# Moving sixteen accumulating transfers of a weight sum from the attention stage into the recurrence stage of a hybrid block

## Chip, cores and metric

The kernel runs on one core of one Trainium2 chip. The metric is the time of one execution on the device in microseconds (us), taken as the median of several runs. All other times are from one profiled execution.

## What is computed

One layer on 1024 tokens of width 1024: a stick-breaking attention (8 heads of 64) and a gated linear recurrence, HGRN2 (4 heads of 128), run on the same normalised input, are merged by two sigmoid gates, and are followed by an MLP and a norm.

```python
xn = rmsnorm(x, norm1_g[layer])
u = xn @ w_in[layer].astype(f32)
q_sb, k_sb, v_sb, f_raw, i_hg, q_hg, g_hg, gate_sb, gate_hg = jnp.split(u, list(c), axis=-1)
o_sb = stick_breaking_attention(...)
o_hg = hgrn2_chunkwise(...)          # state: S_t = diag(f_t) S_{t-1} + k_t v_t^T
o_hg = merge_heads(rmsnorm(o_hg, ...)) * jax.nn.silu(g_hg)
g_a = jax.nn.sigmoid(gate_sb + bg[:D_MODEL])
g_b = jax.nn.sigmoid(gate_hg + bg[D_MODEL:])
merged = g_a * (o_sb @ w_o_sb) + g_b * (o_hg @ w_o_hg)
h = x + merged @ w_out
h = h + jnp.square(jax.nn.relu(rmsnorm(h, norm2_g) @ w_ff1)) @ w_ff2
return rmsnorm(h, final_g)
```

## The kernel before

Products are made in two-way split form: an operand is cast to a high part (`hi_copy`, ScalarE, L157) and the rest is subtracted into a low part (`lo_sub`, VectorE, L162); `three` issues three matmuls of 128 x 512 for one product (L129). The large products use schemes that need sums of blocks of weights. Such a sum is made in DRAM: a transfer that GpSimd issues writes a first block, and later transfers with `accum_op=add` add others to it. There are three generators of such transfers, each yielding after one issue:

- `out_weight_sums`: 32 transfers of 256 KB into `tw`, for the product with w_out (L1365).
- `sb_weight_sums`: 8 transfers of 512 KB into `tv`, for the attention's output product (L1629). Some read what an earlier one wrote.
- `gate_weight_sums`: 16 transfers of 512 KB into `tg4` (called tg in the profile, L1377). For each of four row blocks there is one plain write and then three additions, in four rounds over the four blocks. Eight raw units (`RawUnit`, wga0 to wga7) read tg4 later through SP's queue.

The stages run in this order. The attention loops over 64 `items` (8 heads of 8 query blocks, in the order 7, 0, 6, 1, 5, 2, 4, 3). For an item it issues the scans of the next (`weights`), the scores of the one after that (`scores`, z, with the sigmoid on ScalarE), some steps of the projections, the transposes (`turn`, pw, cast to wTh and wTl) and the products with the values (`values`, po). `turn` also clears a block of wTh and wTl by two GpSimd memsets when the query block is even (L892). At the end of a head GpSimd adds up the two halves of its output (osb, L941). In each item but every sixteenth one transfer of the chained generators `wsums` is issued.

The recurrence follows: for each of 4 heads `hg_levels` is a generator with eight steps, the last seven for the levels 1, 2, 4 ... 64, and `hg_tail` of the head before runs in turns with it. On a level VectorE multiplies keys (k), queries (q) and decays (pp), ScalarE copies the next keys (ksl), and TensorE makes the scores (sl). `hg_level[0]` is the product of the decays on the latest level (`mul(right, right, left)`). Between the steps the stream `st` issues steps of projections: with head 0 it is the product for i (pji, weights wir, wih, wil), whose third and fourth weight parts are split inside level 1, and the weights of f and q of head 3 (wf3, wq3) are loaded and split ahead of their use. The raw buffers of such weights are two in number, so that a load goes out once the part two before it has been split.

All loads from `load` go through SP's queue in a fixed order. `after(a, b)` adds a dependency of issue order only (`NOSYNC`). The program is put in order by a planner, which gives each engine one queue that it works off in order; on one engine nothing overtakes. GpSimd (POOL) has its transfers, memsets and the small norms of `hg_tail` (`inv_rms`, L266) in one queue.

Of the kernel before, what the change touches and what calls it, by code (L numbers as in the profile page):

```python
# [40 lines left out]
def kernel(  # L41
# [19 lines left out]
    nc = tc.nc  # L61
# [32 lines left out]
    def dram(name, shape):  # L94
        return scratch.tile(shape, F32, tag=name, name=name)
# [10 lines left out]
    def after(ins, earlier):  # L106
        if earlier is not None and earlier.ins is not ins.ins:
            tc.add_manual_dep(ins.ins, earlier.ins.name, NOSYNC, reason="issue order")
        return ins
# [710 lines left out]
    turn_lo, scored = [None], [None]  # L820

    def scores(h, qb):
        open_block("main")
        nk = (qb + 1) * P
        QH, QL, KS = qk[h]
        rm = zs[h, qb] = slot_n(f"rm{h}_{qb}", nk)
        step = 320 if nk == 640 else 512
        for s0 in range(0, nk, step):
            m = min(nk - s0, step)
            n = max(m, 256)  # L830
            z = bank(f"z{h}_{qb}_{s0}")
            for i, Q in enumerate((QH, QL)):
                matmul(
                    z[:, :n],
                    Q[:, qb * P : (qb + 1) * P],
                    KS[:, s0 : s0 + n],
                    start=i == 0,
                    stop=i == 1,
                )
            scored[0] = nc.scalar.activation(  # L840
                rm[:, s0 : s0 + m], z[:, :m], AF.Sigmoid, scale=-0.125
            )
# [7 lines left out]
    def weights(h, qb):  # L850

        nk = (qb + 1) * P
        rm = zs[h, qb]
        parts = ((512, nk), (0, 512)) if qb == NT - 1 else ((0, nk),)
        for i, (a, b) in enumerate(parts):
            rr = rm[:, a:b][:, ::-1]
            sc = nc.vector.tensor_tensor_scan(  # L859
                out=rr,  # L860
                data0=rr,
                data1=bits[:, 1024 - nk + a : 1024 - nk + b][:, ::-1],
                initial=rm[:, b : b + 1] if i else 0.0,
                op0=ALU.mult,
                op1=ALU.max,
            )
            if (h, qb) == items[0]:
                after(sc, masked[0])
            if i == 1 or (qb == 5 and h in (2,)):
                after(sc, turn_lo[0])  # L870
# [85 lines left out]
    hg_sum, hg_level = [None], [None]  # L956
# [397 lines left out]
    def out_block(i, j):  # L1354
        return W_OUT[i * 512 : (i + 1) * 512, j * 512 : (j + 1) * 512]

    def out_weight_sums():
        b11, b12, b21, b22 = (out_block(i, j) for i in range(2) for j in range(2))
        plain = ((1, b11), (3, b12), (2, b22), (4, b21))
        summed = ((1, b12), (3, b22), (2, tw[1]), (4, tw[2]))  # L1360
        for op, ways in ((ALU.bypass, plain), (ALU.add, summed)):
            for i, src in ways:
                for r in range(4):
                    rs = slice(r * P, (r + 1) * P)
                    after(nc.gpsimd.dma_start(tw[i][rs], src[rs], accum_op=op), scored[0])  # L1365
                    yield

    tg4 = dram("tg4", [512, D])

    def gate_weight_sums():  # L1370
        for op, i, c0 in (
            (ALU.bypass, 0, C_GA), (ALU.add, 0, C_GB), (ALU.add, 1, C_GA), (ALU.add, 1, C_GB),
        ):
            for r in range(4):
                rs = slice(r * P, (r + 1) * P)
                src = W_IN[i * 512 + r * P : i * 512 + (r + 1) * P, c0 : c0 + D]
                after(nc.gpsimd.dma_start(tg4[rs], src, accum_op=op), scored[0])  # L1377
                yield

    def gate_bias(which, cb):  # L1380
# [150 lines left out]
    def input_sums():  # L1531


        def step(out, a, b, op):
            after(nc.vector.tensor_tensor(out=out, in0=a, in1=b, op=op), turn_lo[0])

        def stored(m, kp, t):
            nc.gpsimd.dma_start(sx[m][kp], t)

        for kp in range(2):  # L1540
            (h00, l00), (h01, l01), (h10, l10), (h11, l11) = (
                [t.bitcast(F32) for t in xn.t[i, 2 * j + kp]] for i in range(2) for j in range(2)
            )
            s = slot(f"xs{kp}")
            step(s, h00, h10, ALU.subtract)
            yield
            step(s, s, l00, ALU.add)
            yield
            step(s, s, l10, ALU.subtract)
            stored(7, kp, s)  # L1550
            yield
            yield
            step(s, s, h11, ALU.add)
            yield
            after(
                nc.vector.scalar_tensor_tensor(
                    out=s, in0=s, scalar=-1.0, in1=l11, op0=ALU.mult, op1=ALU.subtract
                ),
                turn_lo[0],
            )  # L1560
            stored(6, kp, s)
            s4 = slot(f"xs4{kp}")
            yield
            step(s4, s, h01, ALU.add)
            yield
            step(s4, s4, l01, ALU.add)
            stored(3, kp, s4)
            yield
            step(s, s, h00, ALU.add)
            yield  # L1570
            step(s, s, l00, ALU.add)
            stored(5, kp, s)
            yield
# [41 lines left out]
    def sb_block(i, j):  # L1615
        return W_OSB[i * 256 : (i + 1) * 256, j * 512 : (j + 1) * 512]

    def sb_weight_sums():
        for t, op, src in (
            (1, ALU.bypass, sb_block(0, 0)),  # L1620
            (3, ALU.bypass, sb_block(0, 1)),
            (1, ALU.add, sb_block(0, 1)),
            (3, ALU.add, sb_block(1, 1)),
            (2, ALU.bypass, tv[1]),
            (2, ALU.add, sb_block(1, 1)),
            (4, ALU.bypass, tv[2]),
            (4, ALU.add, sb_block(1, 0)),
        ):
            after(nc.gpsimd.dma_start(tv[t], src, accum_op=op), scored[0])  # L1629
            yield  # L1630
# [1005 lines left out]
    n_first = 4  # L2636
    n_fill = n_first + 14 * NHS
    ready = deque()
    wsums = chain(out_weight_sums(), sb_weight_sums(), gate_weight_sums())
    insums = input_sums()  # L2640
    done = 0
    for i, it in enumerate(items):
        if i + 1 < len(items):
            weights(*items[i + 1])
        if i + 2 < len(items):
            st.finish(j_qk[items[min(i + 4, len(items) - 1)][0]])
            scores(*items[i + 2])
        if i < 2:
            v_moves()
        if i % 16 != 0:  # L2650
            next(wsums, None)
        if i > 2 and i % 5 > 1:
            next(insums, None)
        want = n_first + (i + 1) * (n_fill - n_first) // len(items)
        st.advance(want - done, j_q[2])
        done = want
        before = ready.popleft() if ready else None

        def between():
            if before:  # L2660
                values(*before)

        r = turn(*it, between)
        if i == len(items) - 2:
            attended[0] = turn_lo[0]
        if it[1] != NT - 1:
            between()
        if r:
            ready.append(r)
# [9 lines left out]
    for h in range(NHG + 1):  # L2679
        lev = hg_levels(h) if h < NHG else iter(())  # L2680
        tail = hg_tail(h - 1) if h > 0 else iter(())
        upto = (j_i, j_sb[0], j_raw[1], j_raw[6], j_held)[h]
        going, turned = True, False
        while going:
            going = False
            for g in (lev, tail):
                if g is tail and h == 1 and turned and going and st.pos < j_i:
                    continue
                turned = turned or g is tail
                if next(g, StopIteration) is not StopIteration:  # L2690
                    going = True
                    owed += FILL[h]
                    for step in range(int(owed)):
                        st.advance(1, upto)
                        while soon:
                            soon.pop(0)()
                    owed -= int(owed)
        if h + 1 < NHG:
            st.finish(max(j_f[h + 1], j_q[h + 1]))
# [102 lines left out]
```

## Time and profile before

| what | before |
|---|---|
| median of 3 runs | 1420.58 us (1420.08 to 1421.21) |
| profiled execution | 1421.75 us, span 1420.0 us |
| TensorE (PE) | 1406.0 us busy, 99% |
| VectorE (DVE) | 1066.9 us, 75% |
| ScalarE (ACT) | 667.8 us, 47% |
| GpSimd (POOL) | 164.4 us, 12% |
| DMA queue q1 (SP) | 196.15 MB, 40.9% of 16 engines |
| DMA queue q0 (GpSimd's) | 50.34 MB, 13.8% of 16 engines |

The span is that of the program's instructions; the execution has 1.75 us around it. Busy time of PE counts matmuls that run one into the next, so that idle time of PE is true waiting. In a row of instructions the first number is the start, the second the duration (for several, the stretch they cover), and the bracket tells how long the engine was idle before it and what ended that. In the profile tg is written from 252.1 us (first issue) to 302.0 us (last issue), and its first reader is issued at 465.4 us. The attention lasts from about 84 to 330 us.

### The profile page before, as it was taken

The page shows a single profiled execution, that of the slowest core. Times are in us where ns is not written, and L with a number is a line of the kernel's source. Part 1 is how long each engine was busy: PE and PEld are TensorE (multiplying, and loading weights), DVE is VectorE, ACT ScalarE, POOL GpSimd, SP SyncE. Part 2 cuts the span into 40 slices and gives each one's busy share as a digit, 9 for nine tenths or more (in the row PEclk, how much of TensorE's full clock was granted, in tenths as well). Part 3 has the DMA queues.
Part 4 walks back from the last instruction along what each step waited for, and adds up shares of the span by engine and source line. Part 5 has one row for each costly group of instructions (what it writes and reads, how often), then busy time and mean ns, then how long its engine had stood idle before and what let it go on. Part 6 is the DMA issues. An engine that isn't in the chain of part 4 may idle for free.

```text
span 1420.0 us, 18679 instructions
## 1 busy us (share of the span) xinstructions
PE 1406.0 (99%) x6824; PEld 1181.1 (83%) x6824; DVE 1066.9 (75%) x1463; ACT 667.8 (47%) x1147; POOL 164.4 (12%) x318
## 2 busy tenths in 40 slices
PE   9999999999999999999999999999999999999997
PEld 8888788888888888888888888888888888888886
DVE  6678887668578968987788897676666657768765
ACT  6455455554244555433334754445444443433343
POOL 3023343310001111000000300000000000000041
PEclk9999999999999999999999999999999999999999
DMA  7357778864213668364585514444346964776824
GB/s 252 83 141 201 150 142 195 211 149 134 86 56 105 215 222 264 129 215 156 165 294 194 185 59 164 163 163 149 137 143 244 355 255 160 270 278 241 282 91 176
DMA packets 169556, 258.18 MB, mean 182 GB/s; under 512 B 31404, under 2 KB 92376, under 8 KB 169432
## 3 DMA queue, kind: packets, MB, share of 16 engines
q1 hardware_dynamic: 148280, 196.15, 40.9%
q0 software_dynamic: 16320, 50.34, 13.8%
q10 hardware_dynamic: 4864, 10.49, 2.1%
q8 instruction: 54, 0.88, 0.3%
q14 instruction: 38, 0.31, 0.1%
HBM read 186.69 MB, written 84.94 MB: 191 GB/s over the span
## 4 chain that ended last, share of the span: by engine, by line
PE 95%; DVE 1%; ACT 1%; DMA 1%; issue 1%; SPq 0%; POOL 0%; POOLq 0%; DVEq 0%
PE pm L129 21%; PE pX L129 9%; PE pW L129 6%; PE pY L129 6%; PE pjqk L129 5%; PE gY L129 4%; PE gX L129 4%; PE pga L129 4%; PE pjf L129 3%; PE pji L129 3%; PE pyh L129 3%; PE pjq L129 3%; PE pys L129 3%; PE po L129 3%; PE pwX L129 2%; PE z L129 2%
## 5 line engine op out<-in xcount | busy, mean ns | idle before, releaser
L859 DVE TENSOR_TENSOR_SCAN rm<-rm,bits 128x512 f32<-128x512 f32 (+6 forms) x72 | 87.4, 1221 | 29.7 <-ACT rm L840 28.8
L157 ACT CAST whid<-w 128x1024 fp32r<-128x1024 f32 x30 | 31.6, 1054 | 154.1 <-PE pm L129 83.2
L129 PE MATMUL pm<-whid,sh 128*128 128x512 f32 x240 | 93.4, 389 | 0.0
L129 PE MATMUL pm<-wlod,sh 128*128 128x512 f32 x240 | 93.4, 389 | 0.0
L129 PE MATMUL pm<-whid,sl 128*128 128x512 f32 x240 | 93.4, 389 | 0.0
L129 PE MATMUL pm<-tl,sh 128*128 128x512 f32 (+1 forms) x210 | 81.3, 387 | 0.0
L129 PE MATMUL pm<-th,sl 128*128 128x512 f32 (+1 forms) x210 | 81.3, 387 | 0.0
L129 PE MATMUL pm<-th,sh 128*128 128x512 f32 (+1 forms) x210 | 81.3, 387 | 0.0
L162 DVE TENSOR_TENSOR wlod<-w,whid 128x1024 fp32r<-128x1024 f32 x30 | 36.7, 1223 | 53.6 <-ACT whid L157 53.6
L157 ACT CAST wTh<-pw 128x512 fp32r<-128x512 f32 (+2 forms) x96 | 43.8, 483 | 57.9 <-PE pw L132 54.2
L2413 POOL TENSOR_SCALAR fss<-fss 128x1 f32<-128x1 f32 x8 | 4.4, 552 | 562.0 <-ACT fsc L2408 561.5
L162 DVE TENSOR_TENSOR sl<-sa,sh 128x1024 fp32r<-128x1024 f32 x56 | 68.3, 1219 | 0.4 <-ACT sh L157 0.3
L162 DVE TENSOR_TENSOR wTl<-pw,wTh 128x512 fp32r<-128x512 f32 (+2 forms) x96 | 50.4, 546 | 21.8 <-ACT wTh L157 20.7
L157 ACT CAST sh<-sa 128x1024 fp32r<-128x1024 f32 x56 | 57.2, 1046 | 9.0 <-DMA sa<-ad 9.0
L129 PEld LDWEIGHTS pm<-wlod,sh 128*128 128x128 f32 x240 | 45.1, 188 | 9.5
L129 PEld LDWEIGHTS pm<-whid,sl 128*128 128x128 f32 x240 | 45.1, 188 | 9.3
L129 PEld LDWEIGHTS pm<-whid,sh 128*128 128x128 f32 x240 | 45.0, 187 | 9.4
L129 PE MATMUL pX<-sqh,t1l 128*128 128x512 f32 x128 | 49.9, 390 | 0.0
L129 PE MATMUL pX<-sql,t1h 128*128 128x512 f32 x128 | 49.9, 390 | 0.0
L129 PE MATMUL pX<-sqh,t1h 128*128 128x512 f32 x128 | 49.8, 389 | 0.0
L840 ACT ACTIVATE rm<-z 128x512 f32<-128x512 f32 (+3 forms) x96 | 44.5, 501 | 8.4 <-DMA sx<-xs 5.7
L129 PEld LDWEIGHTS pm<-th,sh 128*128 128x128 f32 x210 | 39.5, 188 | 8.1
(985 smaller groups left out, 4415.2 us busy)
## 6 DMA issues: line engine op xcount, KB each, us to landing
w<-in_w_ff_dram SPq DMA_DIRECT2D x72, 512.0 KB, 5.1
sa<-ad SPq DMA_DIRECT2D x52, 512.0 KB, 6.7
tg<-in_w_in_dram POOLq DMA_DIRECT2D x16, 512.0 KB, 9.1
ad<-a SPq DMA_DIRECT2D x32, 256.0 KB, 4.3
ad<-s SPq DMA_DIRECT2D x16, 512.0 KB, 2.8
tw<-in_w_out_dram POOLq DMA_DIRECT2D x24, 256.0 KB, 5.6
pr<-pd SPq DMA_DIRECT2D x10, 512.0 KB
x<-in_x_dram SPq DMA_DIRECT2D x8, 512.0 KB, 11.3
```

The lines of the kernel that those rows point to most:

```text
L129: return pe(nc.tensor.matmul(*a, **k))
L157: hi_last[0] = after(in_turn("act", nc.scalar.copy(dst, src)), hi_behind[0])
L162: nc.vector.tensor_tensor(out=dst, in0=src, in1=hi.bitcast(F32), op=ALU.subtract),
L840: scored[0] = nc.scalar.activation(rm[:, s0 : s0 + m], z[:, :m], AF.Sigmoid, scale=-0.125)
L859: sc = nc.vector.tensor_tensor_scan(out=rr, data0=rr, data1=bits[:, 1024 - nk + a : 1024 - nk + b][:, ::-1], initial=rm[:, b : b + 1] if i ...
L2413: nc.gpsimd.tensor_scalar(out=ssq, in0=ssq, scalar1=1.0 / D, scalar2=EPS, op0=ALU.mult, op1=ALU.add)
```

## The change

`gate_weight_sums` is taken out of the chain that the attention steps through. In the attention, the 40 transfers left are issued in 5 of 8 items and not in 15 of 16. In the recurrence, once a level has made its product of decays, one transfer of tg4 is issued after each step of `hg_levels` (for head 1 after each step of `hg_tail` too), ahead of the projection steps of that turn; its dependency of issue order is on `hg_level[0]` where it was on the latest scores. With eight steps of a head, seven transfers come with head 0 and nine with head 1. The transfers themselves are the same.

```diff
@@ gate_weight_sums
-                after(nc.gpsimd.dma_start(tg4[rs], src, accum_op=op), scored[0])
+                after(nc.gpsimd.dma_start(tg4[rs], src, accum_op=op), hg_level[0])
                 yield
@@ attention
-    wsums = chain(out_weight_sums(), sb_weight_sums(), gate_weight_sums())
+    wsums = chain(out_weight_sums(), sb_weight_sums())
+    gsums = gate_weight_sums()
...
-        if i % 16 != 0:
+        if i % 8 not in (0, 3, 6):
             next(wsums, None)
@@ recurrence
                 if next(g, StopIteration) is not StopIteration:
                     going = True
+                    if hg_level[0] and (g is lev or h == 1):
+                        next(gsums, None)
                     owed += FILL[h]
                     for step in range(int(owed)):
                         st.advance(1, upto)
```

## The prediction

> **What bounds the kernel now.** I read the page first (busy shares and the chain that ended last), then the waits of PE, then busy time by stage, then single stretches of the timeline.
>
> ```profile
> PE 1406.0 (99%) x6824; PEld 1181.1 (83%) x6824; DVE 1066.9 (75%) x1463; ACT 667.8 (47%) x1147; POOL 164.4 (12%) x318
> ...
> q0 software_dynamic: 16320, 50.34, 13.8%
> ...
> PE 95%; DVE 1%; ACT 1%; DMA 1%; issue 1%; SPq 0%; POOL 0%; POOLq 0%; DVEq 0%
> ```
> PE is busy 1406.0 of 1420.0 us and makes 95% of the chain. Only a moment in which PE stands still, or runs at a lower clock, changes the time. The stages (attention 84 to 330, first half of the recurrence 330 to 420) and the waits of PE:
>
> ```profile
> 84.00:330.00 246.00, 243.01 (x1387) 210.00 (x1386) 195.41 (x250) 137.29 (x315) 76.68 (x163) 0.99 0.73 167
> 330.00:420.00 90.00, 90.00 (x475) 76.88 (x474) 64.28 (x115) 34.08 (x73) 2.78 (x4) 1.00 0.27 88
> ...
> PE po L129 <- DVE wTl L162: 2.3, 2, 2.2
> ```
> The columns are the stretch and its length, then busy time (and count) of PE, PEld, DVE, ACT and POOL, then clock, DMA share, GB/s. The attention loses 3.0 us of PE, 2.3 of it to two waits for DVE; the recurrence loses none. The one long wait is this:
>
> ```profile
> 169.32 1.21 DVE L162 TENSOR_TENSOR wqk5l<-wqk5r,wqk5h 128x1024 fp32r<-128x1024 f32 x1
> 170.46 0.87 DVE L162 TENSOR_TENSOR wTl<-pw,wTh 128x512 fp32r<-128x512 f32 x2
> ...
> 171.18 0.39 PE L129 MATMUL po<-wTl,V 128*128 128x256 f32 x1 [2.17 <-DVE wTl L162]
> ...
> 171.00:176.00 5.00, 4.82 (x20) 4.39 (x21) 4.16 (x7) 1.72 (x4) 1.49 (x2) 0.66 0.82 213
> ```
> PE stood for 2.17 us, and in the 5 us behind it the granted clock averaged 0.66, which is 5 x 0.34 = 1.7 us more. So a stall of about 2 us costs about 3.9 in all here. No wait of PE names POOL or a DMA in the attention: the transfers that leave it were hidden there.
>
> **Removed from the attention.** Sixteen issues on POOL and 16 x 512 KB of traffic:
>
> ```profile
> L1377 POOL DMA_DIRECT2D tg<-in_w_in_dram x16: 814/1016/2087, 252.1 to 302.0; - x16
> ...
> DMA to landing us min/median/max: 6.9/9.1/12.8
> ...
> L137 SPq DMA_DIRECT2D wga0r<-tg x1: 448/448/448, 465.4 to 465.4; - x1
> ```
> 16 x 1.0 us leave POOL, which is busy 77 of 246 us there and waited for by nobody on the path: gain 0. If that cover were not there it would show as a wait of PE for POOL, and the list has none in the attention. The first reader of the sums issues at 465.4, on SP's queue; nothing below puts the last sum past 380, so that read and the loads queued behind it on SP lose nothing.
>
> **Moved within the attention.** The 32 issues for tw and 8 for tv now take 40 of the 64 items (5 in 8) where 15 in 16 took the first 42. tw ends near item 50 (only the W_OUT product behind the gates reads it: nothing). tv begins at item 52 and ends at item 63, so its chain of dependent transfers moves from 216-251 to the last head:
>
> ```profile
> 231.36 0.52 POOL L1629 DMA_DIRECT2D tv<-tv  x1 [1.03 <-DMA tv<-in_w_o_sb_dram]
> 239.47 0.91 POOL L1629 DMA_DIRECT2D tv<-in_w_o_sb_dram  x1 [7.58 <-DMA tv<-tv]
> 246.81 0.52 POOL L1629 DMA_DIRECT2D tv<-tv  x1 [4.47 <-DMA tv<-in_w_o_sb_dram]
> 251.02 0.90 POOL L1629 DMA_DIRECT2D tv<-in_w_o_sb_dram  x1 [3.04 <-DMA tv<-tv]
> ...
> 299.77 0.83 POOL L941 DMA_DIRECT2D osb<-osb  x1 [14.73 <-ACT osb L934]
> 300.31 1.15 POOL L1377 DMA_DIRECT2D tg<-in_w_in_dram  x1
> 301.14 1.46 POOL L1377 DMA_DIRECT2D tg<-in_w_in_dram  x1
> 301.98 1.75 POOL L1377 DMA_DIRECT2D tg<-in_w_in_dram  x1
> 326.97 0.82 POOL L941 DMA_DIRECT2D osb<-osb  x1 [16.38 <-ACT osb L934]
> ...
> 322.24 1.44 PE po L129 x12
> ```
> POOL waits in these. Item 58, now the tg at 301.14, becomes the first tv<-tv; with the old spacing (8.1, 7.3, 4.2 us) the second tv<-tv issues at 316.5 and the last add at 320.8. Queued behind the former on POOL are the clears of the last two attention tiles (L892); PE needs them at 322.24, so 5.7 us remain: cost 0, rival 3 if the chain is longer. The osb sum at 326.97 comes after the last add.
>
> **Added to the recurrence: the step that decides.** Each transfer is to come "behind a level's product". That dependency is of issue order. The three rows at 300.31 to 301.98 belong to items 57, 58 and 59, which are 246/64 = 3.8 us apart in PE's work, and POOL took them 0.8 us apart as soon as osb (299.77) had gone: none waited for its own activation. POOL has nothing between osb at 326.97 and the norms of the first head's tail, after 400 us, so the first four transfers go out at about 327.8 to 330, before the first level's product (332.67), and the twelve sums follow as fast as their row's last landing lets them. By bytes, 16 x 0.524 = 8.4 of q0's 50.34 MB, at 13.8% of 1420 us, is 32.7 us of all 16 DMA engines. What those engines do there already:
>
> ```profile
> 326.00:334.00 8.00, 8.00 (x37) 6.61 (x36) 7.96 (x13) 4.83 (x8) 0.82 (x1) 1.00 0.57 135
> 334.00:342.00 8.00, 8.00 (x44) 6.88 (x44) 6.76 (x10) 3.81 (x5) 0.00 (x0) 1.00 0.64 194
> 342.00:350.00 8.00, 8.00 (x41) 6.74 (x40) 7.83 (x15) 2.29 (x4) 0.00 (x0) 1.00 0.33 98
> 350.00:366.00 16.00, 16.00 (x84) 13.67 (x83) 12.01 (x23) 7.36 (x16) 0.00 (x0) 1.00 0.40 149
> ```
> That is 4.6 + 5.1 + 2.6 + 6.4 = 18.7 us of work; with 32.7 more the engines are full from 328 to about 379. Three weight loads fall into it, and they come just in time:
>
> ```profile
> 332.78 0.37 SPq L137 DMA_DIRECT2D wir<-in_w_in_dram  x1
> 334.52 0.37 SPq L137 DMA_DIRECT2D wf3r<-in_w_in_dram  x1
> 338.79 0.37 SPq L137 DMA_DIRECT2D wq3r<-in_w_in_dram  x1
> ...
> 336.26 1.06 ACT L157 CAST wih<-wir 128x1024 fp32r<-128x1024 f32 x1
> 339.21 1.05 ACT L157 CAST wf3h<-wf3r 128x1024 fp32r<-128x1024 f32 x1 [1.90 <-DMA wf3r<-in_w_in_dram]
> ...
> 332.67 0.69 DVE L170 TENSOR_TENSOR pp<-pp 128x512 f32<-128x512 f32 x1
> 337.54 1.22 DVE L162 TENSOR_TENSOR wil<-wir,wih 128x1024 fp32r<-128x1024 f32 x1
> 344.37 0.72 DVE L170 TENSOR_TENSOR q<-q,pp 128x512 f32<-128x512 f32 x1
> ...
> 345.42 1.05 PE L129 MATMUL sl<-q,ksl 128*128 128x128 f32 x8
> ```
> The last wir load lands within 336.26 - 332.78 = 3.5 us. Its cast (ACT) and its wil (DVE) stand in the queues ahead of the level's products; DVE works without a gap from 337.54 to q (ends 345.1), and PE takes that q at 345.42. The slack is 0.2 us before wil and 0.3 before PE, plus whatever the load landed before its cast, for which I choose 0.7 (the row shows no wait of ACT for it): 1.2 in all. What a load loses beside POOL's traffic:
>
> ```profile
> L137 SPq DMA_DIRECT2D wqk4r<-in_w_in_dram x2: 368/476/583, 108.9 to 109.3; - x2
> ...
> DMA to landing us min/median/max: 4.3/4.3/4.3
> ...
> L137 SPq DMA_DIRECT2D wqk6r<-in_w_in_dram x2: 368/610/852, 149.1 to 149.5; - x2
> ...
> DMA to landing us min/median/max: 8.2/8.2/8.2
> ```
> The second pair went out just behind three tw transfers (145.0 to 149.0) and took 3.9 us longer. I take 3.9: it is the same kind of load beside the same kind of traffic. Stall: 3.9 - 1.2 = 2.7 us of PE at the third level, and 1.7 for the clock as at 171: 4.4 us. The ends: nothing (the load gets through first), or 9.1 (a median tg) - 3.5 - 1.2 = 4.4 and 1.7, that is 6.1, and some 2 more if wq3r (issued at 338.79, once wir's buffer is free) adds a stall at the next level. wf3r is late by as much, but what stands behind its cast in ACT's queue (the next level's keys) waits for DVE's k, which is late already: 0. No gain can come from this step, since PE has no idle time there to win.
>
> The Trainium skill, "DMA: Bandwidth & Descriptors", section "Queues, rings and completion order", says that a DMA engine takes turns between its queues, one packet at a time; it speaks against this change. By it, as an estimate, each of wir's 16 packets per engine waits for one of q0's (0.138 x 1420 x 16 / 16320 = 0.19 us): 3.1 us later instead of 3.9, and a sum of 3.6. No view shows single packets; the 8.2 us of wqk6r are of that size. The skill's "TensorE: Matmul & The Clock Gate", "HAM oscillation", puts the gap that lowers the clock at more than about 3.4 us; here 2.17 us was followed by it, so the row is used. By the page the sum would be 2.7, inside the measurement's bound.
>
> **Sum.** The profiled execution: 1420.0 us span, 1421.75 with what lies around it, 1.17 above the median of 1420.58. Span 1420.0 + 0 (attention) + 4.4 = 1424.4; the median becomes 1425.0.
>
> **Rivals.** The least change that a measurement of this kernel can tell is taken as 0.2%, 2.8 us.
> 1. The transfers stay hidden: the loads get through, or stalls stay under 2.8 us, or each transfer really waits for its level, which spreads sixteen over 332 to 394, about 4 us apart, beside DMA shares of 0.33 to 0.64. Then 1420.6. For it: PE had no DMA wait while the same traffic ran in the attention. Against it: there wir was loaded long before its cast, here it is not. 0.37.
> 2. Faster: with sixteen entries fewer, the order in which the queues are planned in the attention comes out differently, and wqk5l no longer stands before wTl at 169.3. It decides if wTl goes first, at once after its cast: 2.2 + 1.7 = 3.9 us, 1416.7, if the recurrence adds nothing. For it: an accident of order is easily undone. Against it: neither instruction has to do with POOL. 0.17.
> 3. The tv chain holds the clears past 322.24: from a chain of over 21 us on. Four us longer than reckoned past that point, and the clock, is 5.7: 1426.3. 0.04.
> My forecast, the late load, has 0.42: between 1423.4 and 1428.6, 1425.0 the middle.
>
> Slower by over 0.2%: 0.42 + 0.04 = 0.46; within: 0.37; faster: 0.17. The range reaches from inside the faster case, 1417.2 (about 0.1 below), to 1428.6, the 8.1 us of the upper ends (0.1 above).
>
> **What would show it.** tg issues from about 328 and not at the levels' times; DMA share over 0.8 from 328 to 370; ACT idle before wih, wf3h or wq3h on a DMA for 3 us and more; PE waiting at an sl or pji matmul near 345 and a clock under 1 behind it. Wrong if PE stays at 90.0 of 90 in the recurrence, or if the time moves at 169 or in another place of the attention, where I hold the order to be as before.

## The result and the profile after

The changed kernel takes 1444.97 us (1444.71 to 1446.28, 5 runs) against 1420.08 us (1419.62 to 1421.21, 5 runs) measured beside it: ratio 1.0176, 95% interval 1.0161 to 1.0191, 24.9 us slower. The direction was the predicted one, and late weight loads are behind it as forecast; the size was 4.4 us in the forecast. The spans, 1442.8 and 1420.0 us, differ by 22.8.

The changed kernel's page, its stages, and PE's waits:

```profile
PE 1408.5 (98%) x6824; PEld 1182.2 (82%) x6824; DVE 1066.4 (74%) x1463; ACT 667.2 (46%) x1147; POOL 166.1 (12%) x318
...
q0 software_dynamic: 16320, 50.34, 13.7%
...
PE 92%; DMA 3%; DVE 2%; ACT 1%; issue 1%; POOL 0%; SPq 0%; POOLq 0%; DVEq 0%; ACTq 0%
```
```profile
84.00:330.00 246.00, 245.46 (x1406) 212.42 (x1405) 199.75 (x255) 139.67 (x317) 66.69 (x150) 1.00 0.61 137
330.00:420.00 90.00, 67.10 (x331) 56.17 (x330) 42.25 (x81) 19.46 (x36) 8.97 (x12) 0.87 0.63 160
```
```profile
PE sl L129 <- DVE q L170: 17.4, 2, 16.4
PE pji L129 <- ACT wih L157: 5.0, 1, 5.0
...
PE po L129 <- DVE wTl L162: 0.5, 2, 0.3
PE pji L129 <- DVE wil L162: 0.5, 1, 0.5
```
DMA has 3% of the chain, where it had 1%. In the recurrence PE is busy 67.1 of 90 us, where it was 90.0 of 90, with the clock at 0.87. Three stalls hold it: 5.0 us for the cast of wir (and 0.5 for wil behind it), 16.4 us for a product q, and 1.0 for the next (17.4 less 16.4). In the attention the 2.2 us at 169 are gone (0.3 is left) and the clock is 1.00. So two things moved, against each other. The osb sum that ends the attention and the first norm of the tail bound the stage:

```profile
321.86 0.82 POOL L941 DMA_DIRECT2D osb<-osb  x1 [3.47 <-ACT osb L934]
322.40 2.41 POOL L1377 DMA_DIRECT2D tg<-in_w_in_dram  x4
329.16 0.84 POOL L1377 DMA_DIRECT2D tg<-in_w_in_dram  x1 [4.35 <-DMA tg<-in_w_in_dram]
...
358.13 0.81 POOL L1377 DMA_DIRECT2D tg<-in_w_in_dram  x1 [1.98 <-DMA tg<-in_w_in_dram]
425.23 0.19 POOL L266 TENSOR_SCALAR hss<-hss 128x4 f32<-128x4 f32 x1 [66.29 <-ACT hon L1288]
```
The same norm before:

```profile
402.66 0.19 POOL L266 TENSOR_SCALAR hss<-hss 128x4 f32<-128x4 f32 x1 [74.86 <-ACT hon L1288]
```
Before, osb went out at 326.97: the attention is now 5.1 us shorter. From there to the norm it was 75.7 us and is 103.4, 27.7 us longer. 27.7 - 5.1 = 22.6, nearly all of the 22.8. Of the 27.7, 22.9 are PE's waits (17.4 + 5.0 + 0.5). Of the other 4.8 about 4 go to the lower clock: from 341 to 347 us PE worked 5.1 us at 0.64, and from 364 to 373 us 7.6 us at 0.71.

The chain of waits, ACT's timeline with the casts, and DVE's timeline show what was late:

```profile
328.30 12.02 DMA wir<-in_w_in_dram
...
342.66 27.15 DMA wq3r<-in_w_in_dram
```
```profile
340.33 1.04 ACT L157 CAST wih<-wir 128x1024 fp32r<-128x1024 f32 x1 [9.13 <-DMA wir<-in_w_in_dram]
360.32 1.04 ACT L157 CAST wf3h<-wf3r 128x1024 fp32r<-128x1024 f32 x1 [18.94 <-DMA wf3r<-in_w_in_dram]
...
369.83 1.05 ACT L157 CAST wq3h<-wq3r 128x1024 fp32r<-128x1024 f32 x1 [7.95 <-DMA wq3r<-in_w_in_dram]
```
```profile
361.39 1.23 DVE L162 TENSOR_TENSOR wf3l<-wf3r,wf3h 128x1024 fp32r<-128x1024 f32 x1 [15.22 <-ACT wf3h L157]
363.62 0.71 DVE L170 TENSOR_TENSOR q<-q,pp 128x512 f32<-128x512 f32 x1
```
wf3, issued at 329.42 on SP's queue, was there at 360.3: 30.9 us, where it took 4.7. wq3 took 27.2 (before, issued at 338.79 and cast at 342.58: 3.8), wir 12.0 (at most 3.5). The weights of wf3 are not used before the third head's product; but their cast and their subtraction stand in the queues of ACT and DVE ahead of the level's q, and PE waits for q. In DVE's timeline before, the same subtraction stood ahead of the same q (344.37) and was in time:

```profile
342.09 1.26 DVE L162 TENSOR_TENSOR wf3l<-wf3r,wf3h 128x1024 fp32r<-128x1024 f32 x1
```

### The profile page after: what moved, and what is told of

It is laid out like the page before. It is cut to its first block, busy times and chain, and to the rows that moved or that the text cites. A ratio compares the mean times of both kernels' runs of the same rounds, so it can differ in the third digit from the quotient of the medians.

```text
span 1442.8 us, 18680 instructions
## 1 busy us (share of the span) xinstructions
PE 1408.5 (98%) x6824; PEld 1182.2 (82%) x6824; DVE 1066.4 (74%) x1463; ACT 667.2 (46%) x1147; POOL 166.1 (12%) x318
## 3 DMA queue, kind: packets, MB, share of 16 engines
q0 software_dynamic: 16320, 50.34, 13.7%
## 4 chain that ended last, share of the span: by engine, by line
PE 92%; DMA 3%; DVE 2%; ACT 1%; issue 1%; POOL 0%; SPq 0%; POOLq 0%; DVEq 0%; ACTq 0%
PE pm L129 21%; PE pX L129 9%; PE pW L129 6%; PE pY L129 6%; PE pjqk L129 6%; PE gY L129 4%; PE gX L129 4%; PE pga L129 4%; PE pjf L129 3%; PE pyh L129 3%; PE pys L129 3%; PE po L129 2%; PE pwX L129 2%; PE pjv L129 2%; PE z L129 2%; PE pji L129 2%
## 5 line engine op out<-in xcount | busy, mean ns | idle before, releaser
L162 DVE TENSOR_TENSOR wTl<-pw,wTh 128x512 fp32r<-128x512 f32 (+2 forms) x96 | 50.3, 546 | 22.6 <-ACT wTh L157 21.4
L129 PEld LDWEIGHTS pm<-tl,sh 128*128 128x128 f32 x210 | 39.4, 188 | 8.1
## 6 DMA issues: line engine op xcount, KB each, us to landing
tg<-in_w_in_dram POOLq DMA_DIRECT2D x16, 512.0 KB, 10.7
```

Of the source, the lines that this page charges most:

```text
L129: return pe(nc.tensor.matmul(*a, **k))
L162: nc.vector.tensor_tensor(out=dst, in0=src, in1=hi.bitcast(F32), op=ALU.subtract),
```

## The experiments

Theory A: the transfers go out in one burst, and while a sum is in POOL's queue, a load of short pieces gets one packet on each DMA engine for each packet of the sum. Theory B: the place alone costs. Theory C: the engines are full, and a load gets what bandwidth is left. The times are medians, and each kernel is compared with the kernel before on the same chip (1420.68 us for the first four, 1420.29 for the other three).

**Each transfer really waits for its level.**
```diff
-after(nc.gpsimd.dma_start(tg4[rs], src, accum_op=op), hg_level[0])
+after(nc.gpsimd.dma_start(tg4[rs], src, accum_op=op), level_done())
...
+def level_done():   # marks: a spare tile, k: a new column; hg_right: the product's first column
+    nc.vector.tensor_copy(marks[:, k : k + 1], hg_right[0])
+    return nc.gpsimd.tensor_scalar(out=marks[:, k + 1 : k + 2], in0=marks[:, k : k + 1], ...)
```
These are the main lines of the edit. This kernel, and the two below that use marks, also give two small tiles (lmx, le) one buffer each.


> Each of the sixteen transfers is held by a real wait: VectorE copies one column of the level's decay product to a spare tile, GpSimd reads it just ahead of the transfer. Theory A (turns by packet: while a sum is in GpSimd's queue, a load gets one packet per engine for each packet of the sum, about 0.35 us, so a load of 64 short packets per engine takes some 22 to 25 us; the harm comes from the sixteen going out in one burst from 322 us): with head 0 only seven go out, four of them plain writes with packets half as long, spread over about 25 us, so wf3 and wq3 land in at most 5 to 12 us instead of 31 and 27; the recurrence loses 0 to 6 us of PE and the time is 1415 to 1422. Theory B (the place alone does the harm: 33 us of DMA work put beside the recurrence's loads, paced or not): the loads are late by about as much as in the changed kernel, 1435 or more.

Measured: 1419.11 us, ratio 0.9992 (0.9983 to 1.0002). From its timeline and its waits of PE:
```profile
329.89 0.55 POOL L965 TENSOR_SCALAR marks<-marks 128x1 f32<-128x1 f32 x1 [6.86 <-DVE marks L964]
330.39 0.57 POOL L1391 DMA_DIRECT2D tg<-in_w_in_dram  x1
336.02 0.56 POOL L965 TENSOR_SCALAR marks<-marks 128x1 f32<-128x1 f32 x1 [5.06 <-DVE marks L964]
336.52 0.56 POOL L1391 DMA_DIRECT2D tg<-in_w_in_dram  x1
```
```profile
PE sl L129 <- DVE q L170: 1.1, 1, 1.1
```
POOL now has a level's mark ahead of each transfer, and the sixteen go out from 330.4 to 394.1 us. wf3 is cast 6.5 us after its issue and wq3 4.8, and PE loses 1.1 us in the recurrence. The same sixteen transfers beside the same levels cost next to nothing once they do what the change says. Theory B falls.

**All sixteen behind head 0's last level.** As above, but with one mark, behind the last level of head 0, and the sixteen issues right behind it:
```diff
+        for _ in gsums if h == 0 else ():
+            pass
```


> All sixteen in one burst, but held by one real wait for the last level product of head 0 (about 350 us), behind the loads of wir, wf3 and wq3. Theory A: no load of short packets is left in the 40 us of the burst that anybody waits for soon (wga9 and osr are read after 390), so PE loses under 1 us in the recurrence and the 5 us that the changed kernel gained in the attention are left: 1414 to 1417, faster than both. Theory B: the burst brings the same 33 us of DMA work into the recurrence, so some stall of 5 us and more comes back: 1420 or more. If the attention's gain of 5 us hangs on where the transfers stand in the recurrence, 1420.

Measured: 1418.0 us, ratio 0.9984 (0.9974 to 0.9993), the fastest of the kernels here, if by less than the 0.2% taken as the bound. The timeline of POOL and the busy time by stretch:
```profile
351.49 0.55 POOL L965 TENSOR_SCALAR marks<-marks 128x1 f32<-128x1 f32 x1 [28.25 <-DVE marks L964]
351.99 2.12 POOL L1392 DMA_DIRECT2D tg<-in_w_in_dram  x4
```
```profile
330.00:350.00 20.00, 20.00 (x105) 17.08 (x104) 17.11 (x31) 7.78 (x12) 0.00 (x0) 1.00 0.56 181
350.00:406.00 56.00, 56.00 (x305) 48.21 (x304) 34.80 (x67) 20.04 (x52) 14.53 (x21) 1.00 0.89 208
```
The DMA engines are busy 0.89 of the 56 us of the burst, and PE never stops. So nearly full DMA engines did no harm here, where no load was wanted soon. The time is 1 us above what was expected: its span (1416.3) is 3.7 under that of before, its median 2.7. The attention is 4.6 us shorter (osb at 322.42), and 0.9 are lost behind the recurrence, in two waits of PE for DVE (0.5 and 0.4).

**The same bytes in pieces of 512 bytes, and of 2 KB.** The changed kernel, with the rows of the transfers cut (c=P for 512 bytes, c=512 for 2 KB) and their pieces taken in reverse, to keep them apart:
```diff
-nc.gpsimd.dma_start(tg4[rs], src, accum_op=op)
+nc.gpsimd.dma_start(tg4[rs].rearrange("p (k c) -> p k c", c=P)[:, ::-1],
+                    src.rearrange("p (k c) -> p k c", c=P)[:, ::-1], accum_op=op)
```


> The changed kernel with the same sixteen transfers and bytes, each row cut into eight pieces of 512 bytes. Theory A: the turn that a load's packet waits for is an eighth as many bytes, about 0.05 to 0.1 us instead of 0.33, so wf3's 64 packets per engine take 5 to 9 us instead of 31 and wq3's as well; the recurrence's loss falls from 23 us to under 8, time 1418 to 1428. Theory C (the engines are simply full, a load gets what bandwidth is left): the bytes are the same and short pieces are no cheaper, so the loads are as late or later: 1440 or more.

> The changed kernel with each row of the sixteen transfers cut into two pieces of 2 KB. Theory A (turns by packet): a turn costs about half of 0.33 us, so wf3 takes 13 to 19 us where rows of 4 KB made it 31 and pieces of 512 bytes at most 13.7; wq3 about 12 to 16; the recurrence loses 8 to 16 us and the time is 1425 to 1435, between the two. Theory C (full engines): no order by the size of the piece, 1440 or more.

Measured: 1423.53 us (1.0022, 1.0013 to 1.0032) with 512 bytes, 1438.3 (1.0127, 1.0112 to 1.0142) with 2 KB, 1444.97 with the whole rows of 4 KB. By the packet records only the twelve additions went out in the smaller pieces; the four plain writes ahead of them still moved in packets of 4 KB. The casts with 512 bytes, then with 2 KB:
```profile
344.12 1.05 ACT L157 CAST wf3h<-wf3r 128x1024 fp32r<-128x1024 f32 x1 [4.14 <-DMA wf3r<-in_w_in_dram]
...
351.19 1.05 ACT L157 CAST wq3h<-wq3r 128x1024 fp32r<-128x1024 f32 x1 [5.50 <-DMA wq3r<-in_w_in_dram]
```
```profile
351.42 1.04 ACT L157 CAST wf3h<-wf3r 128x1024 fp32r<-128x1024 f32 x1 [10.87 <-DMA wf3r<-in_w_in_dram]
363.35 1.04 ACT L157 CAST wq3h<-wq3r 128x1024 fp32r<-128x1024 f32 x1 [10.37 <-DMA wq3r<-in_w_in_dram]
```
From issue to cast wf3 takes 13.7, 21.5 and 30.9 us with pieces of 0.5, 2 and 4 KB; wq3 9.9, 21.5 and 27.2. The transfers themselves got slower with the smallest pieces (17.9 us to landing in the median, 10.7 with whole rows), so the engines were no less loaded, and the loads got through all the same. Theory C, by which the size of the piece changes nothing or worsens it, falls. The packet records tell the same: between 338 and 366 us of the changed kernel there are 1286 packets of the sums, 0.327 us each in the median, and 1400 of the loads; between 346 and 366 with 2 KB they are 1637 of 0.176 us and 1706. That is close to one for one, in both. The 2 KB case lies above its expectation (13 to 19 us for wf3, 1425 to 1435 in time). There a turn of the sums came every 20 us x 16 / 1637 = 0.195 us on an engine, so 64 turns are 12.5 us, and a load also waits for the one ahead of it on SP's queue: wf3 was cast 11.9 us behind wir (339.5), and wq3 11.9 us behind wf3.

**Loads without a wait for a buffer.** The changed kernel, the last two weight parts of i in buffers of their own:
```diff
     u_i.__class__ = ByParts
+    u_i.roomy = (2, 3)
```


> The changed kernel, but the third and fourth weight parts of the product for i get buffers of their own, so that those loads, and those of wf3 and wq3 behind them on the same queue, do not wait for a buffer to be split. Theory A: these loads go out before the burst at 322 us, land in 4 to 9 us each, and the stalls at 336 (5 us) and 347 (16 us) are gone: 1414 to 1420. If it is not the loads' lateness but the burst's work on GpSimd or its use of memory that slows the level's products, the stalls stay: 1435 or more.

Measured: 1436.16 us (1.0109, 1.0093 to 1.0124); the expectation was missed. SP's queue, the cast and PE's wait:
```profile
320.23 0.37 SPq L137 DMA_DIRECT2D wf3r<-in_w_in_dram  x1
...
328.87 0.37 SPq L137 DMA_DIRECT2D wq3r<-in_w_in_dram  x1
```
```profile
354.61 1.04 ACT L157 CAST wq3h<-wq3r 128x1024 fp32r<-128x1024 f32 x1 [23.55 <-DMA wq3r<-in_w_in_dram]
```
```profile
PE sl L129 <- ACT ksl L1102: 15.8, 1, 15.8
```
The time lies in the range of the other case, in which the burst's work on GpSimd or in memory slows the level's products. The trace speaks against that case: the waits of 5.0, 16.4 and 1.0 are gone, and the one wait that stands in their place ends with ksl, which is next behind wq3's cast in ACT's queue. wir and wf3 got ahead of the burst; wq3 still had to wait for a buffer and met it, alone. One load of 512 KB, 25.7 us long, holds PE for 15.8 us; the time is 15.5 above that of before, with the shorter attention already in it. The edit did only a part of what it was made for, but it shows that one such load is enough.

**Why the attention got shorter.** The late burst again, but the other 40 transfers in 15 of 16 items as before the change:
```diff
-        if i % 8 not in (0, 3, 6):
+        if i % 16 != 0:
```


> The late burst again, with the other 40 transfers issued in 15 of 16 items as before the change, so that out of the two edits to the attention only the sixteen transfers' absence is left. If the attention's gain comes of their absence (fewer entries behind which others wait, less traffic), the wait at 169 stays away and the time is that of the late burst, 1417 to 1419. If it comes of the new spacing, by which the planner's order of the queues around item 20 is another one, the wait of 2.2 us and the half clock come back: 1420.5 to 1423.

Measured: 1421.32 us (1.0006, 0.9996 to 1.0015). The wait is back, 2.17 us as before (PE's timeline; in brackets the idle time ahead of the instruction and what ended it):
```profile
170.28 0.39 PE L129 MATMUL po<-wTl,V 128*128 128x256 f32 x1 [2.17 <-DVE wTl L162]
```
So the wait at 169 goes with the new spacing of the other 40, and not with the sixteen being gone. The order on DVE is not what changed. In the changed kernel wqk5l still stands ahead of wTl, and both come 3.6 us earlier:
```profile
165.77 1.21 DVE L162 TENSOR_TENSOR wqk5l<-wqk5r,wqk5h 128x1024 fp32r<-128x1024 f32 x1
166.90 0.87 DVE L162 TENSOR_TENSOR wTl<-pw,wTh 128x512 fp32r<-128x512 f32 x2
```
What made DVE late can be followed back in the trace of before (first fence), beside the late burst with the new spacing (second fence):
```profile
149.03 0.90 POOL L1365 DMA_DIRECT2D tw<-in_w_out_dram  x1
151.26 0.59 POOL L1538 DMA_DIRECT2D sx<-xs  x1 [1.33 <-DVE xs L1535]
...
160.92 0.77 ACT L840 ACTIVATE rm<-z 128x320 f32<-128x320 f32 x2 [5.67 <-DMA sx<-xs]
...
161.72 1.49 DVE L859 TENSOR_TENSOR_SCAN rm<-rm,bits 128x640 f32<-128x640 f32 x1 [4.27 <-ACT rm L840]
```
```profile
151.29 0.57 POOL L1553 DMA_DIRECT2D sx<-xs  x1 [2.17 <-DVE xs L1550]
...
155.61 0.77 ACT L840 ACTIVATE rm<-z 128x320 f32<-128x320 f32 x2 [0.33 <-DMA sx<-xs]
```
sx is another transfer of GpSimd's queue: it stores the tile xs. The tile rm comes from the same pool of buffers as xs (`slot`), and by the profile ACT writes rm only once sx has landed; DVE's scan of rm and all that is behind it in DVE's queue wait for ACT. With the old spacing a third tw goes out at 149, just ahead of sx; with the new one there is none:

| kernel | tw at 149 | sx to landing | ACT waits for sx | PE waits for wTl |
|---|---|---|---|---|
| before | yes | 9.6 us | 5.67 us | 2.17 us |
| late burst, old spacing | yes | 8.7 | 4.79 | 2.17 |
| late burst, new spacing | no | 4.2 | 0.33 | 0.34 |
| changed | no | 3.9 | none | 0.31 |

The two kernels in the middle differ by the spacing alone. So a DMA was behind the one long wait of the attention, two steps behind the engine that PE's wait names.

**The wait at 169 alone.** The kernel before, with wqk5's subtraction put off as that of wqk6 is:
```diff
-                if self.name in ("wf1", "wqk6") or ...
+                if self.name in ("wf1", "wqk5", "wqk6") or ...
```


> The kernel before, with one edit: the low part of wqk5 is put behind the next transposes' low parts (as wf1 and wqk6 have it already), instead of ahead of them. All transfers stay where they were. If the order wqk5l before wTl makes the wait at 169, it and the half clock behind it go: 1416 to 1418, without moving any transfer. If it is the PE's own order that leaves it nothing to do there, the wait moves to another instruction: 1419.5 to 1422.

Measured: 1418.9 us (0.999, 0.998 to 0.9999), between the two cases:
```profile
168.78 0.39 PE L129 MATMUL po<-wTl,V 128*128 128x256 f32 x1 [1.10 <-DVE wTl L162]
```
The wait is halved, and from 165 to 180 us the clock is 1.00 where it was 0.89 before. wqk5l ahead of wTl was half of the wait. The late sx is still there in this kernel (8.3 us to landing, ACT waits 4.37 for it); the changed kernel, which has wqk5l ahead of wTl but no late sx, waits 0.31.

## Why the prediction was right or wrong

- That the transfers do not wait for the levels was right, and decided: four went out at 322.40, as soon as osb had gone. Where they do wait, nothing is lost.
- The place was right in part: late casts, DVE's queue behind them, and a lower clock behind the stall. But wir's late cast stopped PE at pji (5.0 and 0.5 us); the stall at the level's sl, which the prediction gave to wir, came of wf3.
- **The term that failed is the price of a load beside POOL's traffic.** It was put at 3.9 us for wir, from wqk6r against wqk4r, and measured at least 8.5 (12.0 less at most 3.5). By the packet records wir's 16 packets on an engine took 7.4 us, from 332.28 to 339.64, and 2.1 before: 5.2 more, which is 16 x 0.327. The first of them came 4.0 us after the issue, where it was 1.0; why, no run shows. Nor was it "the same kind of load beside the same kind of traffic": wqk6r moves in packets of 256 bytes, wir in 2 KB, wf3 in 512 bytes, and after the three tw transfers the next went out 8 us later (157.07), where here one sum followed the other for 40 us. Nor can a median landing (9.1 us) be the upper end: that is a transfer of 8 packets on an engine, while wf3 has 64, and each takes a turn.
- So "wf3r is late by as much: 0" failed worst. It was late by 26.2 us (30.9 - 4.7), and the stall of 16.4 us is its own: the prediction looked behind wf3's cast in ACT's queue, and not behind wf3l in DVE's, where the q of 344.37 stands. The "some 2 more" for wq3 came out as 1.0: the last packet of the sums went out at 368.3, wq3 was cast at 369.8, and PE had projection steps to do until 371.9.
- The Trainium skill's rule of turns ("DMA: Bandwidth & Descriptors", "Queues, rings and completion order") was the better guide, and the trace agrees with it: 1286 packets of the sums for 1400 of the loads. In the prediction it was worked out for wir alone, with q0's mean packet of 0.19 us, and came out lower than the 3.9. With the sums' 0.327 and wf3's 64 packets an engine it gives 64 x 0.327 = 21 us; wf3 took 30.9, and in the first 10.9 of them wir stood ahead of it, which leaves 20.0.
- The attention at a gain of 0 was wrong by 5.1 us. The step that failed is "no wait of PE names POOL or a DMA in the attention: the transfers that leave it were hidden there". The wait named DVE, and behind DVE stood ACT and a landing in GpSimd's queue. About 4.1 of the 5.1 are there: PE's waits between 161 and 172 us went from 2.8 to 0.3, and the 1.7 of the clock with them. The rival of a remade order named the event, but by luck: the order stayed, the gain came together with the stall and not in its place, and its reason was the spacing of the tw transfers, which the prediction went over at no cost. The prediction's own sign of being wrong, time that moves at 169, came.
- The tv chain held nothing up: the last two transfers issued at 313.36 and 317.51 (316.5 and 320.8 forecast), with the clears gone before, at 306.
- The clock: with gaps of 5.0 and 16.4 us it was 0.64 to 0.71 in the stretches from 341 to 373, about 4 us of PE's work in sum; the forecast had 1.7 for one gap.

## What to carry to other kernels

Before a transfer is moved, ask whether its dependency is a semaphore or only a place in a queue: in another queue, with nothing ahead of it, "behind the level" became "at once". Here a load's time beside another queue was close to its packets on one engine times the other queue's packet, and short rows beside long accumulating rows were the worst of the pairs tried; loads that are just in time are to be checked for it by name. What waits for a late load is whatever stands behind its cast, or behind the subtraction that follows the cast, on any engine, wanted soon or not. And the engine that a wait names is only the last link: follow that engine's own idle time back before you call a transfer hidden.

## What the runs showed of the hardware that was not expected

A load of 512 KB in rows of 512 bytes took 30.9 us from issue to cast beside accumulating transfers in rows of 4 KB (10.9 of them behind another load), 13.7 beside the same bytes in pieces of 512, and 4.7 in the kernel before. The accumulating packet of 4 KB took 0.327 us in the median, a plain one 0.159. A store of 512 KB (sx) took 8.7 us to land with one more transfer just ahead of it in its queue, and 4.2 without. A DMA share of 0.89 over 56 us left PE at 56.0 of 56.
